# A norm's vector moved from the rows to the weights: one change to a hybrid decoder layer on one core

## The chip, the core and the metric

The kernel runs on one core of one Trainium2 chip. A core has a matrix engine (PE in the profile, with its weight loads as PEld), a vector engine (DVE), a scalar engine (ACT), a general engine (POOL) and an engine that issues most transfers (SP). Each engine takes its instructions in a fixed order and waits at semaphores for the others. Data lie in a large on-chip memory, and the matrix engine writes its sums to eight banks of a second one.

The metric is the device time of one execution in microseconds (us). The kernel before takes 999.81 us (median of three runs, 999.69 to 1000.69).

## What is computed

One layer on 1024 rows of 1024 numbers. The part that the change touches is the second half: the row-wise norm with its vector, the up projection, a causal convolution over three rows, a gate, and the down projection.

```python
def rms_norm(x, g):
    xf = x.astype(jnp.float32)
    y = xf * lax.rsqrt(jnp.mean(xf * xf, axis=-1, keepdims=True) + EPS)
    return (y * g.astype(jnp.float32)).astype(x.dtype)
...
    x = x + jnp.concatenate([o_gla, o_swa], axis=-1) @ w_out
    h2 = rms_norm(x, ffn_norm)
    u = causal_dwconv(h2 @ w_up, conv_w, conv_b)
    a, bval = jnp.split(u, 2, axis=-1)
    return x + (jax.nn.silu(a) * bval) @ w_down
```

`w_up` is 1024 x 5632 and `w_down` 2816 x 1024. The vector `ffn_norm` multiplies the columns of `h2`, which are the rows of `w_up`, so it may be applied to either.

## The kernel before

Every product is made in three passes of 128x128 by 128x512 matmuls, on a high and a low part of each operand: `split` (L102) casts the high part on ACT (L104) and subtracts it from the source on POOL or DVE (L107). Large products are cut in two by two blocks and made with seven block products instead of eight (P1 to P7), so the operands are sums and differences of blocks.

**Out projection and second norm.** `o_product` (L817) makes the seven products of a pair of row tiles i and i+4, for i = 0 to 3, and `o_adds` adds them to the rows of x that lie in `acc` (L838). P3 ends tile i and P4 ends tile i+4; then `norm2_stat` takes the sum of squares on ACT (L213), `rms_scale` the factor on DVE and POOL (L176, L178), and `norm2_rows` writes acc times factor times vector on DVE, in two halves (L219). The vector lies in `ffn`, one copy in each partition, loaded by `load_ffn` (512 KB). `norm2_tr` transposes a tile on PE into `big`: tiles 0 to 3 with a high part by L278 and a low part by L286 (or POOL, L229), tiles 4 to 7 at L240, and `norm2_sums` makes the differences with tile t-4 (L255 to L265). The last tiles, 3 and 7, are transposed into banks of the up products, named `fb`.

**Up and down products.** The up weights are taken in 22 chunks of two sides: side 0 for `a`, side 1 for `b`, each 1024 x 128, kept as a tile of 128 x (8 x 128) from a pool of three raw tiles (`load_side`, issued by SP at L898). `up_operand` makes the seven weight operands of a chunk: A11, A12 and A22 are plain parts, S1 to S4 sums made by POOL in the raw tile itself (L910 to L912, L931); chunk 0's sums are made by DVE (`first_sums`). The last operands that read a chunk's raw tiles are S4w (side 0) and A22w (side 1); they free the tiles for the next loads. `product` (L976) multiplies them by the transposed rows. `post` empties the banks: copies on ACT (L1028), sums on DVE (L1036, L1043, L1050), the convolution with one ACT instruction (L988 or L1008) and DVE's multiply-adds (L983, L1010), the gate (L1002 on ACT, L1015 and L1016 on DVE). Two chunks make one pair of the down projection: `down_w` and `down_g` split its weights and gate values (dw, dg in the profile), `down_pair` multiplies six matmuls at a time (L1157) and adds them to `acc` (L1161). One product (12 matmuls) and one such unit alternate on PE from chunk 2 on.

**What sets the order.** The program hands out events with a time (`at`, and `at_us` for those around the up products); they are written out in that order, and a scheduler then places the instructions of each engine. PE's order is pinned to the program's from the first out product to the first up products. The other engines' orders are the scheduler's, but fixed in the built program.

Of the kernel before, what the change touches and what calls it, by code (L numbers as in the profile page):

```python
# [9 lines left out]
F32 = mybir.dt.float32  # L10
# [24 lines left out]
def hymba_layer_kernel(ctx, tc, x, mix_norm, w_in, w_alpha2, b_alpha, gla_norm,  # L35
# [172 lines left out]

    def norm2_stat(t):
        pn, acc = fin["pn"], fin["acc"][t]  # L210
        h = fin["h", t] = pn.tile([P, D], F32, tag="n2h", name=f"n2h_{t}", bufs=2)
        ss = pn.tile([P, 1], F32, tag="n2ss", name=f"n2ss_{t}", bufs=2)
        act.activation(h, acc, AF.Square, accum_out=ss)  # L213
        fin["r", t] = rms_scale(ss, D, 1, f"n2{t}", pn, "n2")

    def norm2_rows(t):
        h, acc, r = fin["h", t], fin["acc"][t], fin["r", t]
        for c in halves:
            dve.scalar_tensor_tensor(h[:, c], acc[:, c], r[:, 0:1], fin["ffn"][:, c],  # L219
                                     op0=ALU.mult, op1=ALU.mult)  # L220

    def norm2_tr(t):
        h = fin["h", t]
        if t < 4:
            b11 = fin["b11"] = fin["pn"].tile([P, 4, 2, P // 2], F32, tag="b11", name=f"b11_{t}", bufs=1)
            tr_hi(t, 0, h, "n2", True)
            act.copy(b11, trs["n2", t, 0])
            if t < 3:
                pool.tensor_sub(tr_dst(t, 0, 1, True), b11, tr_dst(t, 0, 0, True).bitcast(F32))  # L229
            else:  # L230
                tr_lo(t, 0, "n2", True)
            tr_hi(t, 1, h, "n2", True)
            tr_lo(t, 1, "n2", True)
            return
        pbs = fin["pb", t] = []
        for q in range(2):
            pt = bank(f"n2pt_{t}_{q}")
            for k in range(4):
                c = (q * 4 + k) * P
                pe.transpose(pt[:, k * P:(k + 1) * P], h[:, c:c + P], ident)  # L240
            pbs.append(pt.rearrange("p (k c h) -> p k h c", k=4, h=2))

    def norm2_sums(t):

        i, ex = t - 4, fin["ex"]
        p0, p1 = fin["pb", t]

        def put(src, dst, eng=dve):
            dst = dst.rearrange("p k r (h c) -> p k r h c", h=2)
            split(src, dst[:, :, 0], dst[:, :, 1], eng)  # L250

        b12 = fin["h", t][:, 0:512].rearrange("p (k h c) -> p k h c", k=4, h=2)
# [469 lines left out]
    def open_norm2():  # L722
        sh.close()
        w_late["pool"] = swp.enter_context(tc.tile_pool(name="wb", reuse_waits="tile", bufs=1, side="right"))
        fin["sn"] = ExitStack()
        pn = fin["pn"] = fin["sn"].enter_context(tc.tile_pool(name="pn", reuse_waits="tile", bufs=1))
        ffn = fin["ffn"] = pn.tile([P, D], F32, name="ffn")
        fin["s1"] = pn.tile([P, 4, P], F32, name="s1_0")

    def load_ffn():  # L730
        sp.dma_start(fin["ffn"], ffn_norm.partition_broadcast(P).rearrange("p o d -> p (o d)"))

    def open_ff():
        fin["sn"].close()
# [39 lines left out]
        dve.tensor_sub(wo["B11", k2], b22, t2)  # L774

    def load_b21(c2):
        load_gated("B21", 0, c2, fin["pn"].tile([P, D], F32, tag="n2h", name=f"wob21_{c2}", bufs=2))

    def load_b22_late(c2):
        load_gated("B22", 1, c2, fin["pn"].tile([P, D], F32, tag=f"x{c2}", name=f"wob22_{c2}", bufs=1))  # L780
# [34 lines left out]
        sp.dma_start(fin["acc"][t], x[t * P:(t + 1) * P, :])  # L815

    def o_product(name, i):  # L817
        onto = "P1" if name in ("P6", "P5", "P3") else None
        if onto is None:
            psb["o", name, i] = bank(f"o{name}_{i}")  # L820
        pb = psb["o", onto or name, i]
        left = o_left(name, i)
        for k in range(4):
            for n, (ra, rb) in enumerate(PASSES):
                pe.matmul(pb, lhsT=left[:, k, ra, :], rhs=two_streams(ow[name, k][:, rb, :]),  # L825
                          start=(onto is None and k == 0 and n == 0), stop=(k == 3 and n == 2),
                          skip_group_check=onto is not None)

        if (name, i) not in (("P7", 0), ("P7", 1)):
            o_adds(name, i, pb)  # L830

    def o_adds(name, i, pb=None):
        if pb is None:
            pb = psb["o", name, i]
        for dt, half in {"P1": ((0, 0),), "P6": ((4, 0),), "P5": ((4, 1),), "P3": ((0, 1),), "P2": ((0, 0),),
                         "P7": ((4, 1), (4, 0)), "P4": ((4, 0),)}[name]:
            part = fin["acc"][i + dt][:, half * 512:half * 512 + 512].rearrange("p (h c) -> p h c", h=2)
            dve.tensor_add(part, part, halves_of(pb))  # L838
        if name in ("P3", "P4"):
            norm2_stat(i + 4 if name == "P4" else i)  # L840
# [40 lines left out]
    cc = base.tile([P, 4, 44], F32, name="cc")  # L881

    def conv_cols():
        cr = k2_tile("cr")[:44, :].rearrange("p (j c) -> p j c", j=4)
        sp.dma_start(cr[:, 0:3, :], conv_w[0].rearrange("j (c p) -> c j p", p=P))
        sp.dma_start(cr[:, 3, :], conv_b[0].rearrange("(c p) -> c p", p=P))
        fin["cr"] = cr

    def conv_cols_tr():
        pcc = bank("pcc")  # L890
        for i in range(4):
            pe.transpose(pcc[:, i * 44:(i + 1) * 44], fin["cr"][:, i, :], ident[:44, :44])
        dve.tensor_copy(cc, pcc[:, 0:176].rearrange("p (a b) -> p a b", a=4))

    def load_side(ch, sd):
        raw = raws["u", ch, sd] = raw_tile(f"up{ch}_{sd}").rearrange("p (k n) -> p k n", k=KD)
        c0 = sd * DFF + ch * P
        sp.dma_start(raw, w_up[:, c0:c0 + P].rearrange("(k p) n -> p k n", p=P))  # L898
# [514 lines left out]
    at_us(starts[2, 0] - 0.05, open_down_banks)  # L1413
    at_us(-42, load_chunk, 0)
    at_us(-41, load_side, 1, 0)
    for (ch, op), us in (((0, "A11"), EA), ((0, "A12"), EB), ((1, "A11"), -9.8), ((1, "A12"), -9.7),
                         ((0, "S4"), 1.74), ((0, "S1"), 1.75), ((0, "S2"), 1.77), ((0, "S3"), 1.9),
                         ((0, "A22"), 1.91)):
        at_us(us, *((behind,) if us < 0 and ch else ()), up_operand, ch, op)
    at_us(-12, behind, first_sums)  # L1420
    at_us(0.15, norm2_tr, 7)
    at_us(0.29, norm2_sums, 7)
    at_us(1.76, load_side, 1, 1)
    for n, (ch, name, t0) in enumerate(prods):
# [68 lines left out]
```

## Time and profile before

| | us |
|---|---|
| median of three runs | 999.81 |
| profiled execution | 1001.43 |
| its span in the profile | 999.7 |
| PE busy | 974.2 |
| DVE busy | 825.3 |
| POOL busy | 647.5 |
| ACT busy | 500.0 |

The page gives the busy time of each engine, then the span in 40 slices. Each digit is the busy share of a slice in tenths; PEclk is the clock that PE was granted. The rows of PE, DVE, ACT and of that clock:

```profile
PE   8999999999999978999999999999999999999998
DVE  6877767767565798698999989898989899898986
ACT  5637655445454354455454545545454545455451
PEclk9999999999999997999999999999999999999999
```

Slices 15 and 16 (350 to 400 us) stand out: PE works less there, its clock falls, and DVE is full. That is where the second norm lies. Other views used below: the waits of an engine (`engine line <- engine line: us in total, times, longest`), the timeline (start, duration, engine, line, operation, and in brackets the idle time before it and what ended it), and the busy time of each engine in a given stretch.

### The profile page before, as it was taken

The numbers are of one execution on the slowest core, as the hardware profiler recorded it, in microseconds if no ns is written. First come the engines' busy times: TensorE is split into PE (matmuls) and PEld (weight loads), VectorE is DVE, ScalarE is ACT, GpSimd is POOL, SyncE is SP. The second block draws the span as 40 slices with busy tenths as digits, with TensorE's granted clock in tenths as the row PEclk, the third lists the DMA queues.
The fourth block names the chain that finished last, engine by engine and source line by source line (L and its number), as shares of the span: only waits on it lengthen the run. The fifth ranks groups of instructions, "written<-read, shape, count | busy, mean of one in ns | idle before, by whom it ended". The sixth has DMA issues, their size and how long they took to land.

```text
span 999.7 us, 13937 instructions
## 1 busy us (share of the span) xinstructions
PE 974.2 (97%) x4915; PEld 842.5 (84%) x4915; DVE 825.3 (83%) x1368; ACT 500.0 (50%) x1029; POOL 647.5 (65%) x539
## 2 busy tenths in 40 slices
PE   8999999999999978999999999999999999999998
PEld 6888887888888766878888888888888888888887
DVE  6877767767565798698999989898989899898986
ACT  5637655445454354455454545545454545455451
POOL 5592132335575424787879788887888788978750
PEclk9999999999999997999999999999999999999999
DMA  7152223131305101212121221212120212222104
GB/s 228 62 154 70 46 57 87 27 86 64 106 1 189 43 0 43 85 43 64 43 64 42 64 63 50 77 43 85 43 85 22 66 42 63 64 63 64 43 22 169
DMA packets 67541, 68.23 MB, mean 68 GB/s; under 512 B 4651, under 2 KB 52238, under 8 KB 67471
## 3 DMA queue, kind: packets, MB, share of 16 engines
q1 hardware_dynamic: 63484, 62.35, 20.4%
q10 hardware_dynamic: 3986, 4.99, 2.1%
q8 instruction: 39, 0.64, 0.3%
q14 instruction: 32, 0.25, 0.1%
HBM read 58.41 MB, written 4.19 MB: 63 GB/s over the span
## 4 chain that ended last, share of the span: by engine, by line
PE 77%; DVE 9%; POOL 5%; issue 3%; DMA 2%; ACT 2%; ACTq 0%; SPq 0%; POOLq 0%; DVEq 0%
PE fb L976 35%; PE dn_P L1157 17%; PE dg L348 4%; PE dr L348 4%; PE dv L348 3%; PE oP L825 3%; PE pv L534 1%; DVE n2h L219 1%; PE dl L1186 1%; PE fb L1186 1%; PE dq L848 1%; DMA up<-in_w_up_dram 1%; PE go L644 1%; PE ga L635 1%; DMA wob<-in_w_out_dram 1%
## 5 line engine op out<-in xcount | busy, mean ns | idle before, releaser
L1157 PE MATMUL dn_P<-dw,dg 128*128 128x512 f32 x840 | 205.2, 381 | 1.4 <-DVE acc L1161 0.7
L1161 DVE TENSOR_TENSOR acc<-acc,dn_P 128x1024 f32<-128x1024 f32 x140 | 169.3, 1210 | 31.3 <-PE dn_P L1157 31.2
L1157 PEld LDWEIGHTS dn_P<-dw,dg 128*128 128x128 f32 x840 | 157.2, 189 | 27.8 <-DVE acc L1161 3.2
L107 POOL TENSOR_TENSOR dw<-dn,dw 128x512 fp32r<-128x512 f32 x50 | 64.6, 1292 | 35.6 <-ACT dw L104 35.6
L983 DVE SCALAR_TENSOR_TENSOR ua<-fb,cc,ua 128x511 f32<-128x511 f32 (+1 forms) x84 | 61.9, 739 | 1.2 <-ACT ua L988 0.8
L976 PE MATMUL fb<-big,A11w 128*128 128x512 f32 x252 | 58.3, 380 | 1.1 <-ACT e L1032 1.1
L976 PE MATMUL fb<-big,S1w 128*128 128x512 f32 x252 | 58.6, 379 | 0.0
L976 PE MATMUL fb<-big,A12w 128*128 128x512 f32 x252 | 58.1, 379 | 0.0
L976 PE MATMUL fb<-big,S4w 128*128 128x512 f32 x252 | 58.1, 379 | 0.0
L976 PE MATMUL fb<-ex,S2w 128*128 128x512 f32 x252 | 58.0, 379 | 0.0
L976 PE MATMUL fb<-ex,S3w 128*128 128x512 f32 x252 | 57.8, 379 | 0.0
L976 PE MATMUL fb<-ex,A22w 128*128 128x512 f32 x252 | 57.8, 379 | 0.0
L510 POOL TENSOR_TENSOR pr<-pr,sm 128x512 f32<-128x512 f32 x16 | 17.3, 1080 | 61.4 <-DVE sm L509 36.0
L988 ACT ACTIVATE ua<-fb,cc 128x512 f32<-128x512 f32 x42 | 32.7, 778 | 46.6 <-DVE fb L1036 30.1
L976 PEld LDWEIGHTS fb<-big,A11w 128*128 128x128 f32 x252 | 47.5, 189 | 8.2 <-ACT e L1032 1.5
L976 PEld LDWEIGHTS fb<-big,A12w 128*128 128x128 f32 x252 | 47.6, 189 | 6.8
L976 PEld LDWEIGHTS fb<-ex,S2w 128*128 128x128 f32 x252 | 47.6, 189 | 6.8
L976 PEld LDWEIGHTS fb<-ex,S3w 128*128 128x128 f32 x252 | 47.6, 189 | 6.8
L976 PEld LDWEIGHTS fb<-big,S4w 128*128 128x128 f32 x252 | 47.6, 189 | 6.8
L976 PEld LDWEIGHTS fb<-ex,A22w 128*128 128x128 f32 x252 | 47.6, 189 | 6.8
L976 PEld LDWEIGHTS fb<-big,S1w 128*128 128x128 f32 x252 | 47.6, 189 | 6.8
L107 POOL TENSOR_TENSOR A22w<-up,A22w 128x512 fp32r<-128x512 f32 x22 | 30.0, 1364 | 31.6 <-ACT A22w L104 31.6
(487 smaller groups left out, 2571.8 us busy)
## 6 DMA issues: line engine op xcount, KB each, us to landing
up<-in_w_up_dram SPq DMA_DIRECT2D x44, 512.0 KB, 3.8
dn<-in_w_down_dram SPq DMA_DIRECT2D x22, 512.0 KB, 3.5
acc<-in_x_dram SPq DMA_DIRECT2D x8, 512.0 KB, 4.8
out_dram<-acc SPq DMA_DIRECT2D x15, 256.0 KB, 2.1
xt<-in_x_dram SPq DMA_DIRECT2D x7, 512.0 KB, 3.3
vraw<-in_w_in_dram SPq DMA_DIRECT2D x4, 512.0 KB, 3.9
graw<-in_w_in_dram SPq DMA_DIRECT2D x4, 512.0 KB, 4.0
qt<-qt ACTq DMA_DIRECT2D x16, 128.0 KB, 2.2
```

The costliest lines, as they stand in the source:

```text
L107: (eng or pool).tensor_sub(lo, src, hi.bitcast(F32))
L219: dve.scalar_tensor_tensor(h[:, c], acc[:, c], r[:, 0:1], fin["ffn"][:, c], op0=ALU.mult, op1=ALU.mult)
L348: pe.matmul(pb[:, :n], lhsT=big[:, t, k, ra, :], rhs=two_streams(ws[k][:, rb, :n]), start=(k == 0 and i == 0), stop=(k == KD - 1 and i == 2))
L510: pool.tensor_tensor(pr, pr, den[:, hs].rearrange("p (j o) -> p j o", o=1).broadcast_to((P, 4, P)), ALU.mult)
L534: pe.matmul(pbs[i][HALF[g]], lhsT=vv[rows, t - 1 + b, HALF[g]], rhs=rhs[rows, :, HALF[i]], start=start, stop=stop)
L825: pe.matmul(pb, lhsT=left[:, k, ra, :], rhs=two_streams(ow[name, k][:, rb, :]), start=(onto is None and k == 0 and n == 0), stop=(k == 3 a ...
L976: pe.matmul(pb, lhsT=w[:, ra, k, :], rhs=b_operand(bn, k, rb).rearrange("p t (h c) -> p t c h", h=2), start=(onto is None and i == 0), sto ...
L983: dve.scalar_tensor_tensor(dst, src, w, dst, op0=ALU.mult, op1=ALU.add)
L988: act.activation(u[:, a:z], y[:, a:z], AF.Identity, bias=b, scale=w2)
L1157: pe.matmul(pb[:, i], lhsT=g[:, ra, c:c + P], rhs=two_streams(w[:, rb, :]), start=(onto is None and n == 0), stop=(n == 2), skip_group_che ...
L1161: dve.tensor_add(acc, acc, pb.rearrange("p i (c h) -> p i h c", h=2))
L1186: pe.matmul(pb[:, c0:c1], lhsT=g[:, ra, (t % 4) * P:(t % 4 + 1) * P], rhs=two_streams(w[:, rb, c0:c1]), start=(ch == NCH - 2 and i == 0), ...
```

## The change

The vector is no longer multiplied into the rows. It is loaded as eight rows of 128 beside the convolution's coefficients and transposed with them, so that `ffc` holds it as eight columns; the broadcast copy and its load are gone. `scale_side` multiplies each up side in place on ACT, in eight instructions of 128x128, after the side has landed and before its operands are made. `norm2_rows` becomes one scaled copy on ACT. Besides: the row tiles `n2h` get a third buffer; the low parts that POOL made for tiles 0 to 2 (L229), and that of one difference per tile, go to DVE, the latter straight in the bank; P4 of pairs 2 and 3 adds onto P7's bank, and P7's add of that half is left out; the gate of tile 7 is asked for later; and the loads of a chunk's sides are asked for earlier.

```diff
+    cols = edge.tile([P, 24], F32, name="cols")
+    mhalf, ffc = cols[:, 0:16], cols[:, 16:24]
...
-        h = fin["h", t] = pn.tile([P, D], F32, tag="n2h", name=f"n2h_{t}", bufs=2)
+        h = fin["h", t] = pn.tile([P, D], F32, tag="n2h", name=f"n2h_{t}", bufs=3)
...
-        h, acc, r = fin["h", t], fin["acc"][t], fin["r", t]
-        for c in halves:
-            dve.scalar_tensor_tensor(h[:, c], acc[:, c], r[:, 0:1], fin["ffn"][:, c],
-                                     op0=ALU.mult, op1=ALU.mult)
+        act.activation(fin["h", t], fin["acc"][t], AF.Copy, scale=fin["r", t][:, 0:1])
...
-            if t < 3:
-                pool.tensor_sub(tr_dst(t, 0, 1, True), b11, tr_dst(t, 0, 0, True).bitcast(F32))
-            else:
-                tr_lo(t, 0, "n2", True)
+            tr_lo(t, 0, "n2", True)
...
-        dve.tensor_add(t2, p1, b11)
-        put(t2, ex[0][:, i], pool)
-        dve.tensor_sub(p0, b21[:, :, 0], t2)
+        dve.tensor_add(p1, p1, b11)
+        put(p1, ex[0][:, i])
+        dve.tensor_sub(p0, b21[:, :, 0], p1)
...
-    def load_ffn():
-        sp.dma_start(fin["ffn"], ffn_norm.partition_broadcast(P).rearrange("p o d -> p (o d)"))
...
-        onto = "P1" if name in ("P6", "P5", "P3") else None
+        onto = "P1" if name in ("P6", "P5", "P3") else "P7" if name == "P4" and i > 1 else None
...
+            if name == "P7" and i > 1 and half == 0:
+                continue
...
+        sp.dma_start(cr[44:52, 0, :], ffn_norm[0].rearrange("(c p) -> c p", p=P))
...
+        dve.tensor_copy(ffc, pcc[:, 44:52])
...
+    def scale_side(ch, sd, k0, k1):
+        for k in range(k0, k1):
+            part = raws["u", ch, sd][:, k]
+            act.activation(part, part, AF.Copy, scale=ffc[:, k:k + 1])
...
-        at(TR + t + 1.3 if t < 7 else O + 0.75, lambda tt=t: gate_tr(tt, psb.pop(("r", tt))))
+        at(TR + t + 1.3 if t < 7 else O + 1.25, lambda tt=t: gate_tr(tt, psb.pop(("r", tt))))
...
+    for sd in range(2):
+        at_us(-37 + sd, scale_side, 0, sd, 0, 8)
+    at_us(-35, scale_side, 1, 0, 0, 8)
...
+    at_us(4.7, scale_side, 1, 1, 0, 8)
...
-            at_us(prods[n - 2][2] + 0.02, load_chunk, ch + 1)
+            at_us(prods[n - 4][2] + 0.02, load_side, ch + 1, 0)
+            at_us(prods[n - 2][2] + 0.015, load_side, ch + 1, 1)
+            for j in range(2):
+                at_us(prods[n - 2 + j][2] - 0.6, scale_side, ch + 1, 0, 4 * j, 4 * j + 4)
+                at_us(prods[n - 1][2] + 1.2 + 1.5 * j, scale_side, ch + 1, 1, 4 * j, 4 * j + 4)
```

The order of the built programs shows where the new instructions stand. First ACT at the start of the second norm, before the change: the last weight casts of chunk 0 (A12w), then the squares of tiles 0 and 4 (L213, `acc` to `n2h`), then the casts of the transposed tile 0.

```order
L104 CAST A12w_3939<-up_0_3659 128x512
L213 ACTIVATE n2h_3736,n2ss_3737<-acc_3143 128x1024
L213 ACTIVATE n2h_3759,n2ss_3760<-acc_3516 128x1024
L278 CAST big<-n2pt_0_3808 128x4x128
L227 COPY b_0_3807<-n2pt_0_3808 128x512
```

The same place after it (L898 is the multiply of a side, L214 the square, L218 the scaled copy):

```order
L105 CAST A12w_3957<-up_0_3659 128x512
L898 ACTIVATE up_1_3661<-up_1_3661,cols 128x128 x8
L898 ACTIVATE up_0_3680<-up_0_3680,cols 128x128 x8
L214 ACTIVATE n2h_3760,n2ss_3761<-acc_3145 128x1024
L214 ACTIVATE n2h_3782,n2ss_3783<-acc_3518 128x1024
L218 ACTIVATE n2h_3760<-acc_3145,n20r 128x1024
L218 ACTIVATE n2h_3782<-acc_3518,n24r 128x1024
L272 CAST big<-n2pt_0_3829 128x4x128
```

Side 1 of chunk 0 and side 0 of chunk 1 are multiplied between A12w and the squares.

The second place is ACT in the run of up and down products, at the change from chunk 10 to chunk 11; before:

```order
L104 CAST A22w_6418<-up_1_6188 128x512
L104 CAST A11w_6449<-up_0_6421 128x512
L1008 ACTIVATE ub_10_6426<-fb_4120,cc 128x512
L104 CAST dw_3_6453<-T_4_6322 128x512
L104 CAST dg_3_6456<-ub_9_6197 128x512
L104 CAST A12w_6485<-up_0_6421 128x512
L988 ACTIVATE ua_6338<-fb_4119,cc 128x512
```

and after:

```order
L105 CAST A22w_6588<-up_1_6340 128x512
L898 ACTIVATE up_1_6591<-up_1_6591,cols 128x128 x8
L105 CAST A11w_6621<-up_0_6531 128x512
L1008 ACTIVATE ub_10_6594<-fb_4132,cc 128x512
L898 ACTIVATE up_0_6763<-up_0_6763,cols 128x128 x3
L105 CAST dw_3_6625<-T_4_6486 128x512
L105 CAST dg_3_6628<-ub_9_6349 128x512
L898 ACTIVATE up_0_6763<-up_0_6763,cols 128x128 x5
L105 CAST A12w_6665<-up_0_6531 128x512
L988 ACTIVATE ua_6502<-fb_4131,cc 128x512
```

Side 1 of chunk 11 is multiplied behind chunk 10's A22w, and side 0 of chunk 12 around the casts dw and dg of the down projection.

The third place is ACT one chunk later, from chunk 11 to 12; before:

```order
L104 CAST S4w_6612<-up_0_6421 128x512
L1032 COPY e_6559<-fb_4119 128x2
L1028 COPY ca_6530<-fb_4117 128x512
L104 CAST A22w_6638<-up_1_6423 128x512
L104 CAST dw_6_6645<-dn_6237 128x512
L104 CAST dg_6_6648<-ub_9_6260 128x512
L104 CAST A11w_6675<-up_0_6641 128x512
L1008 ACTIVATE ub_11_6652<-fb_4120,cc 128x512
```

and after:

```order
L105 CAST S4w_6794<-up_0_6531 128x512
L1032 COPY e_6739<-fb_4131 128x2
L1028 COPY ca_6710<-fb_4129 128x512
L105 CAST A22w_6824<-up_1_6591 128x512
L898 ACTIVATE up_1_6827<-up_1_6827,cols 128x128 x3
L105 CAST dw_6_6829<-dn_6401 128x512
L105 CAST dg_6_6832<-ub_9_6424 128x512
L898 ACTIVATE up_1_6827<-up_1_6827,cols 128x128 x5
L105 CAST A11w_6863<-up_0_6763 128x512
L1008 ACTIVATE ub_11_6836<-fb_4132,cc 128x512
```

Here the multiplies of side 1 stand around dw and dg, and those of the next side 0 (not shown) behind L1008. This pattern of two chunks repeats from chunk 4 to chunk 20.

More of the change, by code (lines that the diff above doesn't have):

```diff
@@ L73, in hymba_layer_kernel @@
     edge = ctx.enter_context(tc.tile_pool(name="edge", bufs=1, side="right"))
-    mhalf = edge.tile([P, 24], F32, name="mhalf")
+    cols = edge.tile([P, 24], F32, name="cols")
+    mhalf, ffc = cols[:, 0:16], cols[:, 16:24]
     w_keep = ctx.enter_context(tc.tile_pool(name="wa", bufs=1, side="right"))
@@ L260, in norm2_sums @@
         put(p1, ex[1][:, i])
-        t2 = fin["h", t][:, 512:].rearrange("p (k h c) -> p k h c", k=4, h=2)
-        dve.tensor_add(t2, p1, b11)
-        put(t2, ex[0][:, i], pool)
-        dve.tensor_sub(p0, b21[:, :, 0], t2)
+        dve.tensor_add(p1, p1, b11)
+        put(p1, ex[0][:, i])
+        dve.tensor_sub(p0, b21[:, :, 0], p1)
         dve.tensor_add(p0, p0, b21[:, :, 1])
@@ L726, in open_norm2 @@
         pn = fin["pn"] = fin["sn"].enter_context(tc.tile_pool(name="pn", reuse_waits="tile", bufs=1))
-        ffn = fin["ffn"] = pn.tile([P, D], F32, name="ffn")
         fin["s1"] = pn.tile([P, 4, P], F32, name="s1_0")
-    def load_ffn():
-        sp.dma_start(fin["ffn"], ffn_norm.partition_broadcast(P).rearrange("p o d -> p (o d)"))
     def open_ff():
@@ L776, in load_b21 @@
     def load_b21(c2):
-        load_gated("B21", 0, c2, fin["pn"].tile([P, D], F32, tag="n2h", name=f"wob21_{c2}", bufs=2))
+        load_gated("B21", 0, c2, fin["pn"].tile([P, D], F32, tag="n2h", name=f"wob21_{c2}", bufs=3))
     def load_b22_late(c2):
@@ L883, in conv_cols @@
     def conv_cols():
-        cr = k2_tile("cr")[:44, :].rearrange("p (j c) -> p j c", j=4)
-        sp.dma_start(cr[:, 0:3, :], conv_w[0].rearrange("j (c p) -> c j p", p=P))
-        sp.dma_start(cr[:, 3, :], conv_b[0].rearrange("(c p) -> c p", p=P))
+        cr = k2_tile("cr")[:52, :].rearrange("p (j c) -> p j c", j=4)
+        sp.dma_start(cr[44:52, 0, :], ffn_norm[0].rearrange("(c p) -> c p", p=P))
+        sp.dma_start(cr[:44, 0:3, :], conv_w[0].rearrange("j (c p) -> c j p", p=P))
+        sp.dma_start(cr[:44, 3, :], conv_b[0].rearrange("(c p) -> c p", p=P))
         fin["cr"] = cr
@@ L891, in conv_cols_tr @@
         for i in range(4):
-            pe.transpose(pcc[:, i * 44:(i + 1) * 44], fin["cr"][:, i, :], ident[:44, :44])
-        dve.tensor_copy(cc, pcc[:, 0:176].rearrange("p (a b) -> p a b", a=4))
+            n = 44 if i else 52
+            pe.transpose(pcc[:, i * 64:i * 64 + n], fin["cr"][:n, i, :], ident[:n, :n])
+        dve.tensor_copy(cc, pcc[:, 0:256].rearrange("p (a b) -> p a b", a=4)[:, :, 0:44])
+        dve.tensor_copy(ffc, pcc[:, 44:52])
     def load_side(ch, sd):
@@ L1339, in hymba_layer_kernel @@
     at(O + 4.2, open_norm2)
-    at(O + 4.5, load_ffn)
     for k in range(4):
```

## The prediction

> **What bounds the kernel now.** The page first: the span and the share of each engine.
>
> ```profile
> span 999.7 us, 13937 instructions
> PE 974.2 (97%) x4915; PEld 842.5 (84%) x4915; DVE 825.3 (83%) x1368; ACT 500.0 (50%) x1029; POOL 647.5 (65%) x539
> ```
>
> TensorE (PE) is the bound on average, so I ask next where it is not. Busy time by stretch: attention and the first output products; the stretch with the second norm; the steady run of up and down products.
>
> ```profile
> 100.00:340.00 240.00, 237.08 (x1384) 203.42 (x1383) 163.63 (x380) 118.67 (x330) 103.27 (x83) 0.99 0.25 73
> 340.00:395.00 55.00, 44.15 (x208) 36.45 (x207) 48.74 (x76) 29.34 (x55) 20.21 (x19) 0.91 0.07 20
> 430.00:910.00 480.00, 479.49 (x2214) 417.26 (x2215) 438.68 (x557) 240.06 (x409) 390.92 (x289) 1.00 0.20 59
> ```
>
> The columns are PE, weight loads, VectorE (DVE), ScalarE (ACT), GpSimd (POOL) and PE's clock. From 340 to 395 PE is idle for 10.9 us and its clock is 0.91; DVE works 48.74 of 55. There is something to win. From 430 to 910 PE has no idle time, so nothing can be won there, but DVE has only 480 - 438.68 = 41.3 us to spare: something can be lost. The waits of PE say what DVE is late with in the norm, and those of DVE what its spare time is.
>
> ```profile
> PE n2pt L240 <- DVE n2h L219: 5.7, 4, 2.5
> PE fb L274 <- DVE n2h L219: 3.3, 1, 3.3
> PE n2pt L274 <- DVE n2h L219: 1.2, 1, 1.2
> PE oP L825 <- DVE acc L838: 0.6, 1, 0.6
> DVE acc L1161 <- PE dn_P L1157: 28.0, 26, 2.0
> DVE fb L1050 <- PE fb L976: 6.3, 9, 0.7
> ```
>
> The first three are the multiply at L219 that the change removes: 10.2 us. The last two are nearly all of DVE's spare time in the steady run: it waits for PE, hardly ever for ACT.
>
> **What the change removes.** All 16 multiplies of L219, the two adds of P7 onto half 0 for pairs 2 and 3, and seven subtractions on POOL that become seven on DVE. At most, the waits above go (10.2 + 0.6), and what PE lost to its clock: a stretch in which PE worked 1.47 of 3.40 us is followed by one at 0.53.
>
> ```profile
> 374.10:377.50 3.40, 1.47 (x10) 1.20 (x11) 3.40 (x4) 1.81 (x4) 3.40 (x3) 0.96 0.00 0
> 377.50:380.90 3.40, 3.40 (x10) 2.71 (x9) 3.27 (x7) 1.99 (x5) 3.40 (x4) 0.53 0.00 0
> 386.65 4.94 PE L976 MATMUL gb<-big,A11w 128*128 128x512 f32 x12
> ```
>
> The clock's mean of 0.91 over 55 us is about 4 us more. So the best case for this stretch is -15.
>
> The Trainium skill, "TensorE: Matmul & The Clock Gate", Part 1, has PE's clock halved after at least one idle window of about 3.4 us. These rows show it halved after a window with 1.47 us of work, so here a partly idle one was enough, and the measurement decides. By the page the new wait below would cost no clock.
>
> **What it adds.** 352 in-place multiplies of 128x128 on ACT, eight for each of 44 up sides. The nearest row is a column-scaled 128x128 multiply in place:
>
> ```profile
> 171.59 0.40 ACT L630 ACTIVATE s_mid<-s_mid,fac 128x128 f32<-128x128 f32 x1
> 171.90 0.39 ACT L630 ACTIVATE s_mid<-s_mid,fac 128x128 f32<-128x128 f32 x1
> up<-in_w_up_dram SPq DMA_DIRECT2D x44, 512.0 KB, 3.8
> L898 SPq DMA_DIRECT2D up<-in_w_up_dram x44: 367/368/448, 268.9 to 937.9; - x44
> ```
>
> The second starts 0.31 after the first and lasts 0.4, so in a row one costs 0.31 (0.4 if they didn't overlap), a side 2.5 (3.2), a chunk 5.0, and all 109 us. ACT has 500 us free; as work this is covered. But ACT takes its instructions in order, and the first multiply of a side waits for its DMA (3.8 us from issue). Everything behind it on ACT waits too. That is the cost to find, in two places. The row copies on ACT (L218) I take at 1.1, as the square of the same shape (1.06, below); from below 1.0, from above 1.4.
>
> The rest I cost at nothing. The small DMA for the vector stands ahead of the conv columns at about a hundred us, under PE's 237 of 240. The lost 512 KB load frees a queue whose share is 0.07. The two sides multiplied before 300 hold ACT up to 5 us behind the first up DMA (268.9), again under that PE row; if the cover fails it is +5. gate_tr of tile 7, moved behind one more product, may save 0.7.
>
> **Place 1, the second norm.** On ACT the squares of tiles 0 and 4 now stand behind sixteen multiplies.
>
> ```profile
> 334.31 0.99 SPq L898 DMA_DIRECT2D up<-in_w_up_dram  x2
> 340.41 1.06 ACT L213 ACTIVATE n2h<-acc 128x1024 f32<-128x1024 f32 x1 [7.36 <-DVE acc L838]
> 343.34 1.29 PE L274 MATMUL n2pt<-ident,n2h 128*128 128x128 f32 x8 [1.18 <-DVE n2h L219]
> 374.24 1.72 POOL L107 TENSOR_TENSOR ex<-n2h,ex 128x512 fp32r<-128x512 f32 x1
> 378.85 1.28 POOL L107 TENSOR_TENSOR S3w<-up,S3w 128x512 fp32r<-128x512 f32 x1
> 380.15 1.60 SPq L898 DMA_DIRECT2D up<-in_w_up_dram  x2
> ```
>
> The first side lands at 334.3 + 3.8 = 338.1. Sixteen at 0.31 end at 343.1; two squares (2.1) and the copy (1.1) follow; PE's transposes of tile 0 start at 346.3, not 343.3: +3.0, and about 1.7 for the half clock after it. Then the removed waits pay back: of the 5.7 about 3.2 (tile 6 still waits some 2.5 for a bank; P7's stays taken until P4 is added), the 0.6, the 0.7, and the 3.3 of tile 3. PE is through with tile 3 at about 381 in place of 386.6. There the next wait is ready: the cast of tile 3 stands behind the eight multiplies of side (1,1). Its DMA was issued at 380.15, behind POOL's S3w; two 1.7 us subtractions leave POOL ahead of it, so 376.7, landed 380.5, multiplied 383.0, cast 383.6. That is 3.0 earlier than 386.65. But the low half of tile 3 waits for the multiplies of side (2,0), a square and two copies on ACT and one DVE subtraction: 383.6 + 0.5 + 2.5 + 1.1 + 1.2 + 0.7 = 389.6. The last four of P1's twelve matmuls need it (0.9, or 1.8 at half clock): P1 ends at 390.5 to 391.4, before at 386.65 + 4.94 = 391.6. **Place 1: -0.5**, between -15 (nothing new is late) and +5 (the 3.0 + 1.7 go through).
>
> **Place 2, the steady run.** The work repeats every two chunks; here it is from chunk 10 to 12. ACT casts, POOL's last readers of the raw sides, the DMA issues they free, and DVE:
>
> ```profile
> 663.45 0.63 ACT L104 CAST A22w<-up 128x512 fp32r<-128x512 f32 x1
> 664.15 1.45 POOL L107 TENSOR_TENSOR A22w<-up,A22w 128x512 fp32r<-128x512 f32 x1 [0.24 <-ACT A22w L104]
> 659.88 6.12 SPq L898 DMA_DIRECT2D up<-in_w_up_dram  x2
> 666.91 0.61 ACT L104 CAST dw<-T 128x512 fp32r<-128x512 f32 x1
> 667.41 0.62 ACT L104 CAST dg<-ub 128x512 fp32r<-128x512 f32 x1
> 668.07 0.69 DVE L107 TENSOR_TENSOR dg<-ub,dg 128x512 fp32r<-128x512 f32 x1
> 670.06 0.78 ACT L988 ACTIVATE ua<-fb,cc 128x512 f32<-128x512 f32 x1 [1.50 <-DVE fb L1043]
> 671.06 0.74 DVE L983 SCALAR_TENSOR_TENSOR ua<-fb,cc,ua 128x511 f32<-128x511 f32 x1
> 683.23 0.62 ACT L104 CAST S4w<-up 128x512 fp32r<-128x512 f32 x1
> 685.33 4.24 SPq L898 DMA_DIRECT2D up<-in_w_up_dram  x2
> 687.17 0.62 ACT L104 CAST A22w<-up 128x512 fp32r<-128x512 f32 x1
> 687.93 1.22 DVE L1161 TENSOR_TENSOR acc<-acc,dn_P 128x1024 f32<-128x1024 f32 x1 [1.98 <-PE dn_P L1157]
> 688.46 0.61 ACT L104 CAST dg<-ub 128x512 fp32r<-128x512 f32 x1
> L910 POOL TENSOR_TENSOR S<-up x18: 1274/1369/1818, 446.2 to 907.6; 128x512 f32<-128x512 f32 x18
> ```
>
> Even chunk. Side (11,1), issued at 659.9, lands at 663.7, so behind A22w's cast its eight multiplies run from 664.0 to 666.5 (a cast holds ACT for 0.5: dw at 666.91, dg at 667.41). A11w's cast and L1008 follow to 667.7. Now ACT meets side (12,0). Its DMA waits for POOL's A22w (ends 665.6) and lands at 669.4: ACT stands still. Three multiplies, then dw and dg: dg's high part is ready at 671.4, not 668.0. DVE does L1010 meanwhile and waits about 2.2. Five more multiplies and A12w's cast, then L988 at 673.4 in place of 670.06: DVE's L983 at 674.2 in place of 671.06. DVE is 3.1 late.
>
> Odd chunk. ACT's S4w cast stands behind two things that come from that late DVE, so 683.2 becomes 686.2; POOL's part and the DMA issue go from 685.3 to 688.2; the side lands at 692.0. ACT, done with A22w at about 689, stands still again; three multiplies, dw, dg: 694.0 in place of 689.1. DVE, 3.1 late, skips its 1.98 of waiting for PE, is free at 690.2 and waits 3.8 for dg. Four shorter waits for L1008 and L988 that come late (0.65, 0.4, 0.5, 0.6) make 2.1.
>
> So DVE waits 2.2 + 3.8 + 2.1 = 8.1 in two chunks. A chunk lasts (907.6 - 446.2) / 17 = 27.1, and 480 us hold 8.85 pairs; DVE's spare time is 41.3 / 8.85 = 4.7 a pair. It lacks 3.4. The first 3 or so cost PE nothing, as DVE frees its banks that much ahead of use. From chunk 4 to 20 there are eight pairs: 8 x 3.4 - 3 = +24. Counting the two long waits alone, 6.0 - 4.7 = 1.3, it is 8 x 1.3 - 3 = +7.5. I take the middle, as the short waits are near what such a walk can resolve: **+16**.
>
> **Sum.** -0.5 + 16 = +15.5 on the profiled execution, which took 1001.43, its span of 999.7 and 1.7 around it: 1016.9. It stands 1.6 above the median shown, 999.81, so there: 1015.3, say **1015**. Its own range is 1005 to 1028.
>
> **Rivals.**
> 1. *The scales are swallowed in the steady run and the norm gets its gain.* One mechanism: the up sides land before ACT reaches their multiplies. It decides if side (12,0) lands by 667.7, 1.7 us sooner than worked out, and the odd one by 689. For it: its load is asked for earlier in the program, and three sides can be held. Against: the raw tile is freed by POOL's A22w and S4w as before. Then place 2 is nothing and place 1 is near the half of its best: -7.5, 992. Chance 0.19.
> 2. *DVE waits as said, but at the times at which it waited for PE* (28.0 + 6.3 us are there), and place 1 gives back what it gains: -0.5, 999.3; to ±2. Chance 0.18.
> 3. *A partly idle window doesn't halve the clock*, as the page named above has it, and DVE absorbs its waits. Then the 1.7 behind the 3.0 goes, and as much at P1: rival 2 less 3, 996. The rows with 1.47 of 3.40 speak against it. Chance 0.03.
> 4. *The work isn't moved as said.* The order shows L219 gone and the multiplies in place; no chance of its own.
>
> **Chances.** The forecast has 0.60. 0.2% of this time, 2 us, is about what a measurement of this kernel can tell from no change. Faster by more: rivals 1 and 3, 0.22; within it: rival 2 less its edges, 0.17; slower: 0.61. The range from 996 to 1028 leaves out most of rival 1 and what lies above 24 + 5.
>
> **What would show it.** Right: in the steady run waits of DVE's dg (L108) and L983 for ACT of some 8 us a pair, ACT idle before L898 with the up DMA as releaser, PE idle 3% or more from 450 on; in the norm PE's tile 0 at about 346. Wrong: PE still 479 of 480 there, or no ACT idle before L898. If the new dg waits are short, the sides landed earlier than 3.8 us behind POOL's last reader; if they are long and PE doesn't idle, DVE's lead over PE was larger than 3.

## The result, and the profile after

The changed kernel takes 1046.13 us (median of four runs, 1044.34 to 1050.41); the kernel before, on the same chip, 999.91. The ratio is 1.0467, 95% interval 1.0432 to 1.0502: slower by 46 us. The forecast was 1015 with a range up to 1028: the direction came true, and the place, but not the size.

The page of the profiled execution (1044.34) has the span and the busy time of each engine:

```profile
span 1042.6 us, 14252 instructions
PE 987.9 (95%) x4915; PEld 851.1 (82%) x4915; DVE 824.6 (79%) x1358; ACT 601.0 (58%) x1389; POOL 640.7 (61%) x532
```

ACT is busy 101 us longer, with the multiplies, and still only for 58% of the span. No other engine has a larger share than before, and yet the span is 42.9 us longer. Nothing here has run out of capacity; something waits. The same two stretches as before the change, with the same columns, say where:

```profile
340.00:395.00 55.00, 42.93 (x208) 36.45 (x207) 37.10 (x66) 45.19 (x93) 10.69 (x13) 0.94 0.14 39
430.00:910.00 480.00, 458.06 (x2069) 394.82 (x2068) 420.55 (x526) 290.99 (x636) 368.53 (x271) 0.98 0.17 53
```

From 430 to 910 PE was busy 479.49 of 480; now it is busy 458.06, at a clock of 0.98. DVE works less in the same time too, 420.55 for 438.68. Both stand more. The chain of work that ended last, by engine, shows who holds them; first before the change, then after:

```profile
PE 77%; DVE 9%; POOL 5%; issue 3%; DMA 2%; ACT 2%; ACTq 0%; SPq 0%; POOLq 0%; DVEq 0%
```

```profile
PE 38%; DVE 28%; ACT 14%; DMA 8%; POOL 6%; issue 4%; SPq 0%; ACTq 0%; POOLq 0%; DVEq 0%
```

A kernel whose end was set mostly by PE (77%) is now set by a ring of PE, DVE, ACT and DMA. The waits of PE over the whole span, and then those of DVE and ACT from 430 to 910, close that ring:

```profile
PE dn_P L1157 <- DVE acc L1161: 22.2, 13, 2.4
...
DVE dg L108 <- ACT dg L105: 38.7, 15, 4.2
DVE ub L983 <- ACT ub L1008: 10.8, 8, 2.0
DVE acc L1161 <- PE dn_P L1157: 2.6, 6, 0.5
...
ACT up L898 <- DMA up<-in_w_up_dram: 37.5, 19, 3.3
```

Read from the bottom: ACT stands 37.5 us in front of the multiplies (L898) for a transfer; DVE waits 38.7 us for the cast of dg that stands behind them on ACT, and 10.8 for the copy of L1008; its 28.0 us of waiting for PE have shrunk to 2.6; and PE waits 22.2 us for DVE to free the banks of the down projection.

One such place, at the change from chunk 11 to 12, in the timeline of ACT, of SP and of DVE:

```profile
711.38 0.62 ACT L105 CAST A22w<-up 128x512 fp32r<-128x512 f32 x1
715.20 0.99 ACT L898 ACTIVATE up<-up,cols 128x128 f32<-128x128 f32 x3 [3.20 <-DMA up<-in_w_up_dram]
...
716.60 0.61 ACT L105 CAST dg<-ub 128x512 fp32r<-128x512 f32 x1
...
711.32 2.44 SPq L893 DMA_DIRECT2D up<-in_w_up_dram  x2
...
717.25 1.35 DVE L108 TENSOR_TENSOR dg<-ub,dg 128x512 fp32r<-128x512 f32 x1 [4.16 <-ACT dg L105]
```

SP issues the load at 711.32, when POOL has read the tile for the last time. ACT is through with A22w at 712.00 and meets the first multiply of that side: it stands 3.20 us. The data that dg's cast needs had long been there; it waits because it is behind.

How the lateness grows is read from the first matmul of each chunk's first product (A11w) on PE: chunk 2 and chunk 20, before and then after:

```profile
430.51 1.78 PE L976 MATMUL fb<-big,A11w 128*128 128x512 f32 x7 [1.10 <-ACT e L1032]
...
917.79 1.46 PE L976 MATMUL fb<-big,A11w 128*128 128x512 f32 x6
```

```profile
437.79 1.49 PE L976 MATMUL fb<-big,A11w 128*128 128x512 f32 x3
...
957.89 2.32 PE L976 MATMUL fb<-big,A11w 128*128 128x512 f32 x10
```

7.3 us late at chunk 2, 40.1 at chunk 20. Such rows of chunks 4 and 20 (481.12 to 917.79 before, 489.74 to 957.89 after) give eight pairs: 54.6 us a pair before, 58.5 after, +3.9. The first of them, from chunk 4 to 6, costs 3.6 already.

### The profile page after: what moved, and what is told of

It is laid out like the page before. It is cut to its first block, busy times and chain, and to the rows that moved or that the text cites. A ratio compares the mean times of both kernels' runs of the same rounds, so it can differ in the third digit from the quotient of the medians.

```text
span 1042.6 us, 14252 instructions
## 1 busy us (share of the span) xinstructions
PE 987.9 (95%) x4915; PEld 851.1 (82%) x4915; DVE 824.6 (79%) x1358; ACT 601.0 (58%) x1389; POOL 640.7 (61%) x532
## 4 chain that ended last, share of the span: by engine, by line
PE 38%; DVE 28%; ACT 14%; DMA 8%; POOL 6%; issue 4%; SPq 0%; ACTq 0%; POOLq 0%; DVEq 0%
PE fb L976 9%; DMA up<-in_w_up_dram 6%; DVE ua L983 6%; ACT up L898 5%; PE dn_P L1157 5%; DVE acc L1161 5%; PE dg L342 4%; PE dr L342 4%; DVE dg L108 4%; PE dv L342 3%; PE oP L815 3%; DVE ub L983 2%; ACT dw L105 2%; DVE ub L1140 2%; DVE ub L1016 2%
## 5 line engine op out<-in xcount | busy, mean ns | idle before, releaser
L1157 PE MATMUL dn_P<-dw,dg 128*128 128x512 f32 x840 | 210.4, 388 | 26.7 <-DVE acc L1161 22.2
L1157 PEld LDWEIGHTS dn_P<-dw,dg 128*128 128x128 f32 x840 | 160.1, 192 | 55.6 <-ACT S4w L105 21.1
L1161 DVE TENSOR_TENSOR acc<-acc,dn_P 128x1024 f32<-128x1024 f32 x140 | 168.8, 1209 | 5.3 <-PE dn_P L1157 4.9
L898 ACT ACTIVATE up<-up,cols 128x128 f32<-128x128 f32 x352 | 109.9, 390 | 57.0 <-DMA up<-in_w_up_dram 48.2
L108 POOL TENSOR_TENSOR dw<-dn,dw 128x512 fp32r<-128x512 f32 x50 | 69.2, 1384 | 72.8 <-ACT dw L105 69.6
L108 DVE TENSOR_TENSOR dg<-ub,dg 128x512 fp32r<-128x512 f32 x40 | 44.8, 1120 | 44.5 <-ACT dg L105 43.3
L988 ACT ACTIVATE ua<-fb,cc 128x512 f32<-128x512 f32 x42 | 32.5, 776 | 53.5 <-DVE fb L1036 51.2
L976 PE MATMUL fb<-ex,S3w 128*128 128x512 f32 x252 | 63.2, 404 | 0.0
L976 PEld LDWEIGHTS fb<-ex,S3w 128*128 128x128 f32 x252 | 52.0, 206 | 8.8
L910 POOL TENSOR_TENSOR S<-up 128x512 f32<-128x512 f32 x21 | 26.9, 1281 | 43.2 <-ACT up L898 32.7
```

Of the source, the lines that this page charges most:

```text
L108: (eng or pool).tensor_sub(lo, src, hi.bitcast(F32))
L898: act.activation(part, part, AF.Copy, scale=ffc[:, k:k + 1])
L910: eng.tensor_add(s1, a21, a22)
L976: pe.matmul(pb, lhsT=w[:, ra, k, :], rhs=b_operand(bn, k, rb).rearrange("p t (h c) -> p t c h", h=2), start=(onto is None and i == 0), sto ...
L988: act.activation(u[:, a:z], y[:, a:z], AF.Identity, bias=b, scale=w2)
L1157: pe.matmul(pb[:, i], lhsT=g[:, ra, c:c + P], rhs=two_streams(w[:, rb, :]), start=(onto is None and n == 0), stop=(n == 2), skip_group_che ...
```

## The experiments

All runs are compared with the kernel before on the same chip. My theory: the multiplies cost by their place on ACT, in front of casts and copies that DVE waits for, not by their work; and the moved gate costs by itself.

**1. The gate put back.**

```diff
-        at(... else O + 1.25, lambda tt=t: gate_tr(...))
+        at(... else O + 0.75, lambda tt=t: gate_tr(...))
```

> The change with the gate of tile 7 asked for at its old place, all else as changed. The changed kernel's trace has a wait of 4.9 us of PE for tile 7's gated row (oP for DVE vg) at 298 to 303 and the product behind it at half clock (4.51 in place of 2.75). Theory: that wait is the moved gate's alone, so 5 to 6 us go: 1040 to 1041. Rival: it comes from ACT being held up by the first side's multiplies at 268 to 274; then it stays, within 1 us of 1046.

Measured: 1041.34, ratio 1.0427 (1.0399 to 1.0454): 4.8 us less than the change. The reverse, the gate's move alone in the kernel before:

> The kernel before with one part of the change alone: the gate of tile 7 asked for behind one more product. Theory (the gate's transposes hold back the first P7 on PE's pinned order and half a clock window follows): +4 to +6 us, 1004 to 1006. Rival (the 4.8 us that taking it back saved came from an interplay with the multiplies ahead of 300 us): within 1 us of before, 1000.

Measured: 1004.81 against 999.3, ratio 1.0053 (1.0033 to 1.0073): +5.5. The move costs by itself. PE's timeline shows how; first before the change, with DVE's last instruction of that gate (L683), then after it:

```profile
296.85 0.66 PE L667 MATMUL ogt<-ident,gs 128*128 128x128 f32 x4 [0.67 <-POOL gs L661]
297.26 5.43 PE L825 MATMUL oP<-ex,big 128*128 128x512 f32 x24
302.53 5.34 PE L825 MATMUL oP<-oP7w,big 128*128 128x512 f32 x24
...
302.31 0.68 DVE L683 TENSOR_TENSOR vg<-vg,ogt 128x512 f32<-128x512 f32 x1
```

```profile
289.38 8.02 PE L815 MATMUL oP<-ex,big 128*128 128x512 f32 x36
297.24 0.60 PE L661 MATMUL ogt<-ident,gs 128*128 128x128 f32 x4
302.69 4.51 PE L815 MATMUL oP<-ex,big 128*128 128x512 f32 x12 [4.86 <-DVE vg L677]
307.04 2.32 PE L815 MATMUL oP<-oP7w,big 128*128 128x512 f32 x10
```

The 12 matmuls that wait are P1 of pair 3. They multiply rows of tile 3 and don't read the gate's result: before the change they were the second half of the 24 at 297.26, so they began near 300 and were through at 302.7, and DVE finished the gate only then (302.31 + 0.68). What they wait for is a bank. The eight banks come from two pools of four. `bank` (L55) gives the gate's transposes one from either pool, by whether the number of banks asked for so far is odd or even, and each P1 always one from the first pool. Asked for one product later, the gate falls on the other pool: with three P1 it fills the first one, and the fourth P1 stands until DVE has read the gate's bank for the last time (L677). In the built program the two share a bank; before the change they don't. So PE waits 4.86 us, and its next 12 matmuls take 4.51 in place of 2.75, at a granted clock of 0.55 to 0.66. P7 begins 4.5 us later. The time of the gate alone is the expected one; the reason expected, that the transposes hold back P7, is not the one in the rows.

**2. No multiplies in the steady run** (`scale_side` for chunks 2 and up taken out, so the norm's vector is left out of these chunks; the gate as in the change).

```diff
-                at_us(prods[n - 2 + j][2] - 0.6, scale_side, ch + 1, 0, 4 * j, 4 * j + 4)
-                at_us(prods[n - 1][2] + 1.2 + 1.5 * j, scale_side, ch + 1, 1, 4 * j, 4 * j + 4)
```

> The change without the multiplies of the sides from chunk 2 on (their vector is left out). Theory: all of the loss behind 440 us comes from these multiplies, some 36 us: 1008 to 1012, and a pair of chunks lasts 54.4 again. Rival: a part comes from the earlier loads or from P4 on P7's bank; then over 1015.

Measured: 1003.86, ratio 1.0046 (1.0031 to 1.0061): 42.3 us less than the change, more than expected. The whole loss of the steady run belongs to the multiplies: a pair lasts 54.5 us again, with the earlier loads and P4 on P7's bank still there. It doesn't yet say whether to their work or to their place.

**3. The same work, another place.** A dependency holds the multiplies of a side 0 on ACT until the casts S1w and S3w of the chunk ahead are through; the gate is put back here and in all that follow.

```diff
-                at_us(prods[n - 2 + j][2] - 0.6, scale_side, ch + 1, 0, 4 * j, 4 * j + 4)
+                at_us(prods[n - 2 + j][2] - 0.6, scale_side, ch + 1, 0, 4 * j, 4 * j + 4,
+                      ("up_operand", ch, ("S1", "S3")[j]))
```

> As e1, and the multiplies of side 0 held on ACT until S1w and S3w of the chunk before are cast (four behind each), where ACT was idle; the same 352 multiplies. Theory (ACT stands still for the side's DMA with dg and L988 queued behind it): the wait of the even chunk goes, about 2.2 + 0.4 + 0.6 of 8.1 a pair, and with it the late S4w: 12 to 25 us less than e1, 1016 to 1028. Rival (the amount of work on ACT, 5 us a chunk, is what DVE waits for): the same work, so within 3 us of e1.

Measured: 1019.66, ratio 1.0206 (1.0189 to 1.0223), 21.7 us less than with the gate alone put back. Then, in addition, side 1 asked for later, and in every second chunk held behind the casts dw and dg:

```diff
-                at_us(prods[n - 1][2] + 1.2 + 1.5 * j, scale_side, ch + 1, 1, 4 * j, 4 * j + 4)
+                at_us(prods[n][2] + 0.2 + 0.1 * j, scale_side, ch + 1, 1, 4 * j, 4 * j + 4,
+                      ("down_g", (ch + 1) // 2 - 2, 6) if ch % 2 and ch > 2 else None)
```

> As e3, and side 1 of an even chunk behind the casts dw and dg that stood between its multiplies. Theory: the long wait of DVE for dg goes too; the pair is back near 54.4 and the time within 10 us of the kernel before: 1000 to 1010. Rival (amount of work): within 3 us of e1.

Measured: 1013.38, ratio 1.0140 (1.0124 to 1.0155), a little over the expected range. DVE's waits for ACT from 430 to 910, for the two runs (lines behind `scale_side` are 7 higher, so L1015 is L1008 of the change):

```profile
DVE dg L108 <- ACT dg L105: 32.1, 17, 4.7
...
DVE ub L990 <- ACT ub L1015: 7.2, 8, 1.0
```

```profile
DVE ub L990 <- ACT ub L1015: 18.6, 16, 2.3
...
DVE dg L108 <- ACT dg L105: 2.5, 9, 0.3
```

Free dg, and the copy of L1008 is what stands behind the multiplies: a wait takes the place of the one removed. So side 1 must go behind that too.

**4. Both sides out of the way.** Side 1 behind the L1008 copy, for even chunks behind dg as well:

```diff
-                at_us(prods[n - 1][2] + 1.2 + 1.5 * j, scale_side, ch + 1, 1, 4 * j, 4 * j + 4)
+                at_us(prods[n][2] + 0.2 + 0.1 * j, scale_side, ch + 1, 1, 4 * j, 4 * j + 4,
+                      (("down_g", ch // 2 - 1, 3) if ch % 2 == 0 else ("post", ch, "P7")) if ch > 1 else None)
```

> As the run with all groups later, but with sides (1,0) and (1,1) left where the change has them, so its difference to that run is what place 1 alone gains by the later multiplies. Theory: 999 to 1006, 3 to 5 us above it. Rival (place 1 gains nothing by it): the same time.

In the second kernel the two sides of chunk 1 are moved in the norm as well:

```diff
-    at_us(-35, scale_side, 1, 0, 0, 8)
+    at(O + 7 + 0.5 * 2 + 0.006, scale_side, 1, 0, 0, 8, ("norm2_rows", 4))
-    at_us(4.7, scale_side, 1, 1, 0, 8)
+    at_us(4.7, scale_side, 1, 1, 0, 8, ("norm2_rows", 7))
```

> All multiplies kept, each group placed on ACT behind the last instruction that DVE or PE waits for soon: side 0 behind the casts S1w and S3w, side 1 behind the bank copy of L1008 and (even chunks) behind dg, side (1,0) behind the row copy of tile 4, side (1,1) behind that of tile 7; gate back. Theory (only ACT standing at the multiplies costs; their work is covered): the 6 to 7 us that the run with both sides later still lost in the steady run go, and place 1 gains 3 to 5: 996 to 1003. Rival A (the work of 109 us itself on ACT, or the memory traffic of it beside DVE, costs): 1008 or more. Rival B (place 1 has nothing to gain because the rows need the two products after it anyway): 1001 to 1004.

Measured: 1001.0 for the steady run alone (ratio 1.0015, 0.9999 to 1.0031) and 999.05 for both (0.9995, 0.9977 to 1.0012). With all 352 multiplies on ACT a pair of chunks takes 54.4 us in the first, no more than before the change: rival A, that the work itself costs, is out. The norm gains about 2 us of the 3 to 5 expected, and the two intervals overlap. What place 1 is worth without any multiply, in a kernel that leaves the vector out altogether:

```diff
     def scale_side(ch, sd, k0, k1):
-        for k in range(k0, k1):
+        for k in ():
```

> The change without any multiply on the up sides (the norm's vector is left out of the computation), gate back: what place 1 is worth without its cost. Theory (the multiplies cost both at place 1 and in the steady run, and the removed waits of DVE's L219 pay back up to 10): 988 to 994. Rival (the gain at place 1 is small because tile 0's chain and the last tiles wait for other things): 997 to 1000.

Measured: 994.38, ratio 0.9941 (0.9922 to 0.9959), just above the range that the theory gave (988 to 994).

**5. The last stand removed, and two controls.** In the second kernel of experiment 4 ACT stood once more, 3.5 us in front of the last chunk's side 1. It goes behind that chunk's A12w cast and is asked for later:

```diff
-                at_us(prods[n][2] + 0.2 + 0.1 * j, scale_side, ch + 1, 1, 4 * j, 4 * j + 4,
+                at_us(prods[n][2] + (0.2 + 0.1 * j if ch + 1 < L else MM + 1.4), scale_side, ch + 1, 1, 4 * j, 4 * j + 4,
+                      (("up_operand", L, "A12") if ch + 1 == L else
...
```

> As the run with all groups later, and the last chunk's side 1 placed behind its A12w cast too, ahead of which ACT stood 3.5 us in that run's trace (DVE waited 2.5 us for L1008 there, and the stretch from chunk 20 to the end took some 2 us more than before). Theory (every loss left is such a stand): 996 to 998. Rival (what is left, 4.7 us above the run without any multiply, is the multiplies' own work on ACT): no change, 999.

And with side 0 in one piece:

```diff
-                      ("up_operand", ch, ("S1", "S3")[j]))
+                      ("up_operand", ch, "S3"))
```

> As the run with the last chunk later, but all eight multiplies of side 0 in one piece behind S3w, not four behind S1w and four behind S3w. Theory (DMA has landed by then, so the place no longer matters): within 2 us of that run. Rival (a piece of 2.5 us on ACT holds a cast that DVE needs): 2 to 5 us more.

Measured: 996.41 (0.9967, 0.9952 to 0.9981) and 998.51 (0.9980, 0.9962 to 0.9997) against 1000.5. Both beat the kernel before, by 0.3% and 0.2%; they are 2.1 us apart with intervals that overlap, so they can't be told apart. The first is the best full version of this study. Its group of the multiplies on the page, beside that of the change, with their busy time, mean, and the idle time ahead of them:

```profile
L901 ACT ACTIVATE up<-up,cols 128x128 f32<-128x128 f32 x352 | 110.7, 391 | 8.6 <-DMA up<-in_w_up_dram 5.3
```

```profile
L898 ACT ACTIVATE up<-up,cols 128x128 f32<-128x128 f32 x352 | 109.9, 390 | 57.0 <-DMA up<-in_w_up_dram 48.2
```

The work is the same to 1%; the standing fell from 57.0 us to 8.6, and the time from 46.2 us above the kernel before to 4.1 below it (5 of these 50 us are the gate's). In that run DVE waits for PE again, as before the change (from 430 to 960), and the chain is PE's:

```profile
DVE acc L1168 <- PE dn_P L1164: 31.1, 28, 2.5
```

```profile
PE 73%; DVE 13%; ACT 4%; DMA 4%; POOL 4%; issue 2%; ACTq 0%; DVEq 0%; POOLq 0%; SPq 0%
```

The other control has the gate back and side 1 where experiment 4 puts it, and leaves side 0 as the change has it:

> Gate back, side 1 behind the bank copy of L1008 or dg, side 0 where the change has it (it then stands in front of A12w and L988 of every chunk, and of dw and dg in half of them). Theory (each side alone, placed ahead of what DVE waits for, makes ACT stand): 1010 to 1030. Rival (side 1 ahead of dw and dg, the 3.8 us wait of the odd chunk, is all of it): 1000 to 1004.

Measured: 1049.8, ratio 1.0499 (1.0478 to 1.0520): worse than with the gate alone put back, outside the expected range. With side 1 moved behind L1008 it meets side 0 there, and up to sixteen multiplies stand in one block ahead of A12w and L988 (L995 here). DVE's waits from 430 to 960:

```profile
DVE ua L990 <- ACT ua L995: 43.7, 26, 2.7
DVE dg L108 <- ACT dg L105: 16.5, 9, 2.8
```

These are 60.2 us of waiting, though ACT stood only 22.7 us for the transfers there: in front of an instruction that DVE needs, the block's own work (2.45 us for eight multiplies) counts as well. So no side has a price of its own: experiment 3 without side 0 in the way cost 20, this one without side 1 in the way 49, both away less than 2. What counts is what stands behind the block.

A fourth raw tile, with which loads could start a side earlier, does not fit in the memory beside the rest, so what it would bring stays open.

## Why the prediction was right, and where it was wrong

**The mechanism was right, and the size of three terms was not.** The steady run was put at +16 and cost 32.8; the moved gate was put at -0.7 and cost 4.5; the run-up to chunk 2 and the end were put at nothing and cost 3.3 and 2.8. Place 2 came as said: ACT stands at L898 for the side's transfer, dg, L1008 and L988 come late behind it, DVE uses up its spare time and PE loses what is left over. Of the signs named beforehand, ACT's idle time before L898 is there, and PE is idle for 21.9 of 480 us (4.6%); DVE's waits for ACT came to 6.2 us a pair instead of some 8, and tile 0 came at 351.09 instead of 346, later by the gate's 4.5. In the odd chunk the wait was worked out as 3.8 us and measured as 4.16 at 717.25 (3.8 to 4.2 in every pair).

**Rivals 1 and 2 are out** by the waits: the sides do not land early (19 stands of ACT), and DVE's waits are not absorbed (22.2 us of PE's waiting for L1161). Rival 3's condition, that DVE absorbs its waits, falls with rival 2. With the multiplies elsewhere (experiment 5) rival 1's state was reached, and took 4.1 us off the kernel before, of the 7.5 that it had priced.

**Where the size went wrong.** The span's 42.9 us, by the rows above:

| stretch | predicted | measured |
|---|---|---|
| the gate, to P7 of the first pair | -0.7, hidden | +4.5 |
| from there to the end of chunk 0's P1 | -0.5 | -0.6 |
| from there to chunk 2 | 0 | +3.3 |
| chunk 2 to 20 | +16 | +32.8 |
| chunk 20 to the end | 0 | +2.8 |

*The gate.* "gate_tr of tile 7, moved behind one more product, may save 0.7" looked at the 0.67 us that PE waits ahead of the transposes. Which bank the moved transposes would take, and who needs that bank next, was not asked. Experiment 1 answers it: the next P1 needs it, and stands 4.86 us.

*"I take the middle, as the short waits are near what such a walk can resolve."* The walk through two chunks gave DVE 3.4 us too little per pair; +16 came from averaging its sum, 24, with the 7.5 of the case in which only the two long waits count, so about 2 a pair. The measured pair is 3.9 longer. Where that goes is read over the eight pairs exactly, before and after:

```profile
481.12:917.79 436.67, 436.67 (x2017) 379.73 (x2016) 401.66 (x505) 216.98 (x369) 359.05 (x265) 1.00 0.20 58
489.74:957.89 468.15, 446.56 (x2017) 385.36 (x2016) 409.57 (x504) 284.10 (x625) 362.60 (x265) 0.98 0.18 55
```

DVE's idle time goes from 35.01 / 8 = 4.4 us a pair to 58.58 / 8 = 7.3, which is 2.9 more; 6.2 of the 7.3 are waits for ACT, not the 8.1 of the walk (the even chunk's dg waits about 0.8 in place of 2.2). The other 1.0 is work: DVE's busy time goes from 50.2 to 51.2 a pair, and the prediction had no term for that. So the short waits did count, and that the walk's 3.4 lies so near to 3.9 is partly luck: its waits were too long, and the longer work made up for it.

Seen from PE, the same 31.5 us are 21.6 of idle time and 9.9 of the same matmuls at a clock of 0.98 instead of 1.00, to which the prediction gave no time here. They are not a second loss. In five of the eight pairs half clock follows PE's wait, in three it doesn't, as in these two places:

```profile
564.63 1.79 PE L1157 MATMUL dn_P<-dw,dg 128*128 128x512 f32 x6 [2.30 <-DVE acc L1161]
566.21 4.23 PE L976 MATMUL fb<-ex,S3w 128*128 128x512 f32 x12
...
857.33 1.53 PE L1157 MATMUL dn_P<-dw,dg 128*128 128x512 f32 x6 [2.39 <-DVE acc L1161]
858.70 2.75 PE L976 MATMUL fb<-ex,S3w 128*128 128x512 f32 x12
```

The three pairs without it have a second wait of 1.14 to 1.16 us for L1161 instead, and all eight pairs last 58.2 to 58.7: DVE sets their length.

*"The first 3 or so cost PE nothing."* In the eight pairs nothing was hidden: that from chunk 4 to 6 already took 3.6 us longer. Whether a lead was used up ahead of chunk 4, where chunks 2 to 4 lost only 1.3, is not shown. And the pattern was counted for eight pairs, while chunks 2 to 4 (1.3), the run-up to chunk 2 (3.3) and the end (2.8) paid as well.

With the walk's own 3.4 for eight pairs, nothing subtracted, and the gate at +5, as the prediction priced its failed cover for the multiplies ahead of 300, the forecast would have been about 1032: still 14 low, of which the stretches around the pattern are some 7 and the 0.5 that a pair was longer than 3.4 another 4. The rest, 3, is that the medians lie 46.2 us apart and the profiled spans 42.9.

**Place 1 was right almost to the tenth, for what it covered.** Relative to the gate's 4.5, PE ends P1 of chunk 0 0.6 us early (0.5 predicted), by the wait that was named. (One step of that walk, PE through with tile 3 "at about 381", doesn't come out of its terms, which give 383.5; nothing hung on it, as the low half of tile 3 came last.)

```profile
351.09 1.97 PE L268 MATMUL n2pt<-ident,n2h 128*128 128x128 f32 x8 [4.16 <-ACT n2h L218]
...
388.00 1.99 PE L976 MATMUL gb<-big,A11w 128*128 128x512 f32 x8 [1.65 <-ACT big L272]
394.26 1.28 PE L976 MATMUL gb<-big,A11w 128*128 128x512 f32 x4 [4.26 <-DVE big L280]
395.33 4.33 PE L976 MATMUL gb<-big,A12w 128*128 128x512 f32 x12
```

Tile 0 was forecast at 346.3 and begins at 351.09, of which 4.5 is the gate's. The low half of tile 3 (L280) is late behind side (2,0), as said: on ACT the square of tile 7 (L214) follows seven of its multiplies, and DVE, which has the factor of tile 7 (L177) ahead of L280, waits for it:

```profile
391.63 0.15 DVE L177 TENSOR_SCALAR n27v<-n2ss 128x1 f32<-128x1 f32 x1 [2.48 <-ACT n2h L214]
...
393.52 0.69 DVE L280 TENSOR_TENSOR big<-fb,big 128x512 fp32r<-128x512 f32 x1
```

But the wait's price did not end there: the next product, A12w, took 4.33 for 2.75 before, at a granted clock of 0.50 and then 0.77. That is 1.6 of the 3.3 us lost on the way to chunk 2; the rest wasn't traced. Half clock follows PE's waits of 4.16, 4.26 and 4.86 us here, and not that of 1.65. The rule named in the prediction (the Trainium skill, "TensorE: Matmul & The Clock Gate", Part 1: half clock after an idle window of about 3.4 us) agrees with these four. The steady run speaks against it: there half clock follows five waits of 1.98 to 2.40 us, and doesn't follow three of 2.15 to 2.39. So does the row quoted in the prediction, half clock behind a window that was only partly idle. What decides between waits of the same length is not shown.

**Why 46 us for so little work.** Of the 110 us of multiplies all but 3 or less hide in an engine that is half idle, if they stand where nobody waits: experiment 5 ends at a ratio of 0.9967, the kernel without any multiply at 0.9941. Put a few instructions too early, each block hands the wait for its transfer, and some of its own work, to DVE, which had 4.4 us to spare in 54.6. What DVE lost beyond its waits, the longer work, is only seen, not tried (last section).

## What to carry to other kernels

An instruction that waits for a transfer holds up everything behind it on its engine, however empty that engine is: before adding one, list what stands behind it and who waits for that, and put it behind the last such instruction. When a walk through a repeating pattern gives a loss per round, use the walk; averaging it down, or granting a lead that no row shows, has to be earned by a row. And when an event is moved past another, ask which buffer it then takes, and who needs that buffer next.

## What the runs showed of the hardware

DVE's and POOL's parts of a split (L108), both on tiles in the large memory, slow each other where they overlap. In the changed kernel dw and dg are cast back to back behind a stand, so POOL's part of dw and DVE's part of dg often start almost together. DVE's view and then POOL's, with two such meetings: in the first POOL starts first, in the second DVE:

```profile
717.25 1.35 DVE L108 TENSOR_TENSOR dg<-ub,dg 128x512 fp32r<-128x512 f32 x1 [4.16 <-ACT dg L105]
...
725.09 0.68 DVE L108 TENSOR_TENSOR dg<-ub,dg 128x512 fp32r<-128x512 f32 x1
```

```profile
716.78 1.28 POOL L108 TENSOR_TENSOR dw<-dn,dw 128x512 fp32r<-128x512 f32 x1 [3.41 <-ACT dw L105]
...
725.11 1.80 POOL L108 TENSOR_TENSOR dw<-dn,dw 128x512 fp32r<-128x512 f32 x1
```

The one that starts first keeps its time (POOL 1.28, DVE 0.68), the other takes longer (DVE 1.35, POOL 1.80), by about the time for which the two overlap: as if only one of them were served at a time. The Trainium skill, "GPSIMD Engine Reference", 1. Specifications, says that POOL shares its interfaces to this memory with VectorE and names instructions with two inputs there as those that collide; these rows agree. Over the eight pairs 17 of DVE's 32 instructions of this kind take 1.34 to 1.36 us, where 8 of 32 did before, and their sum is 6.9 us larger (34.4 for 27.5), most of the 7.9 by which DVE's work grew. That the meetings are the cause is an inference, as no run separated them.
